# The skewed bias is loaded ahead of the queries, by every eighth partition; the layer norms' features move by 64 bytes, the first 128 in a tile of their own

## The chip, the cores and the metric

The kernel runs on one core of a Trainium2 chip. The metric is the device time of one execution in microseconds (us), the median of three runs. The profile comes from one more execution that the hardware profiler recorded. Its engines are PE (TensorE, matmuls; PEld is its weight loading), DVE (VectorE), ACT (ScalarE), POOL (GpSimd) and SP (SyncE, here only an issuer of DMAs).

## What is computed

One layer of a decoder trunk over 256 tokens of width 2048, in float32. Three steps, each followed by a layer norm of the scaled input plus the step's result:

```python
h = x
mix = hybrid_mixer(h, w_in, w_out, ...)            # S5 | stick-breaking | NSA heads, then w_out
h = layer_norm(ALPHA * h + mix, ln_g[0], ln_b[0])
xa = memory_cross_attention(h, mem, wq, wkv, wo)
h = layer_norm(ALPHA * h + xa, ln_g[1], ln_b[1])
ff = conv_ffn(h, ffn_w_up, conv_w, conv_b, ffn_w_down)   # 2048 -> 2 x 5632 -> 2048
h = layer_norm(ALPHA * h + ff, ln_g[2], ln_b[2])
```

Two places of it matter here. The 16 NSA heads add a relative-position bias to their scores before the softmax. It depends on query minus key and on the head alone:

```python
def head_bias(dist):
    return tab[t5_bucket(dist)].reshape(*dist.shape, n_g, n_r).transpose(2, 3, 0, 1)
s_w = einsum('bqgrd,bkgd->bgrqk', qb, kwb) * scale + head_bias(dist_w)
```

And the output of the first two layer norms is the input of the next projections: of `wq` (2048 to 512) and of `w_up` (2048 to 11264).

## The kernel before

**Products.** Every large product is taken in three matmuls of a rounded float32: a number is split into `hi` (rounded) and `lo` (the rest), and hi·hi, hi·lo and lo·hi are added up in PSUM. Weights come in chunks of 128 x 1024 (512 KB). SyncE loads each into `raw` (four buffers). ScalarE casts it to `hi` (L285), VectorE subtracts for `lo` (L286), with three buffers each. TensorE reads them in `mm3` (L300 to L302: hi with the high features, hi with the low ones, lo with the high ones), where the weights are the 128 x 128 stationary operand and 256 tokens of features the moving one. `mm3x` (L308 to L310) has the roles the other way round, features stationary and up to 512 weight columns moving. `to_rows` makes one tile of 128 outputs from two chunks: 16 blocks k of 128 features, 48 matmuls in a row. The up-projection is 88 such tiles, the query projection 4.

**Features.** In the mixer the features are the split input `A`. From the first layer norm on they are the four tiles mix0 to mix3, of four blocks each, high and low (`features`); block k is in tile k // 4. The names in rows leave the number out: all four read `mix`. The layer norms write them by `split_on_pe`: TensorE transposes 128 columns of the normalised rows into PSUM, ScalarE casts them (high), TensorE subtracts that in PSUM, ScalarE casts again (low). The same memory holds mixer outputs before, and kept weight chunks in the down-projection. Where a tile begins within a partition follows from the sizes of the pools in front of it. `gap` allocates a few bytes that nothing reads, to shift what comes after. hi and lo begin 32 bytes past a multiple of 128, mix0 and mix1 too, A, mix2 and mix3 96 past one.

**The skewed bias.** `g_dr` in DRAM holds for each head its bias as a row of 384 numbers over the distance. The slab is that bias for 128 queries at once, partition p shifted by p: 128 partitions x 16 heads x 256 numbers, 2 MB. Eight DMAs on ScalarE's queue (L962), each for 16 neighbouring partitions, load it at the start of `nsa`. There it gets memory of its own in a pool that opens after the S5 part is over. `nsa` goes over four quads of heads and two branches. For each head it multiplies queries `nq` with keys `kh`, `kl` (L995, L996), VectorE adds the slab in a reduction that gives the minimum too (L999, L1001, with `mn`), adds the bias of the compressed keys (`tcs`, L1007), and ScalarE takes the exponential (`pe`, L1011). Scores lie in `mx`, two PSUM buffers.

**Order.** A scheduler sets the order of instructions on each engine ahead of time. The program gives it lanes of priority (`lane`: "first", "split", "mixer", "proj", "late"), and `after` forces single pairs. So work of several phases is mixed: around 215 us the last S5 output matmuls (`pa` from `Es`, `Ec`), key projections (`kh`, L926) and, after them, the S5 gelu on `s5u` (L753), its split `s5zs` (L293), the gate product with `w_glu` (16 blocks of 3 matmuls on `s5zs`), then query projections (`nq`, L947). Each engine works its list strictly in order, and a DMA that waits on ScalarE's queue holds what stands behind it. DMAs of both queues take turns at eight completion semaphores, so that an issue also waits for the landing of the transfer that used its semaphore before.

## Time and profile before

| | us |
|---|---|
| median of three runs | 1310.14 (1310.13 to 1311.78) |
| the profiled execution | 1312.0 |
| its span in the trace | 1310.2 |
| PE busy | 1266.3 |
| DVE busy | 882.8 |
| ACT busy | 659.6 |
| DMA, mean over the span | 181 GB/s |

The span is the time from the first to the last instruction in the trace. Busy times of different engines overlap. A matmul's record runs from its start to its modelled end, longer than the distance to the next one; so a pace is read as the distance of starts. A row's last part, in brackets or behind the bar, is the time that the engine idled before it and what ended that. PEclk is the granted clock of TensorE as a share of full speed.

### The profile page before, as it was taken

How to read it: one execution, taken by the hardware profiler on the slowest of the kernel's cores; microseconds unless marked ns; L12 is line 12 of the kernel's file. 1: busy time of each engine (PE TensorE's matmuls, PEld its weight loads, DVE VectorE, ACT ScalarE, POOL GpSimd, SP SyncE). 2: the span in 40 equal slices, each digit the busy share in tenths (PEclk: the TensorE clock that was granted, in tenths of full speed). 3: DMA queues.
4: the chain of work that ended last, by engine and by line, in shares of the span. 5: the costliest groups of instructions: out<-in, count | busy, mean ns of one | idle time of the engine just before them, and what ended most of it. 6: DMA issues, size and time to landing. Idle time of an engine off the chain costs nothing.

```text
span 1310.2 us, 23007 instructions
## 1 busy us (share of the span) xinstructions
PE 1266.3 (97%) x9221; PEld 1172.5 (89%) x9221; DVE 882.8 (67%) x1510; ACT 659.6 (50%) x1030; POOL 13.3 (1%) x23
## 2 busy tenths in 40 slices
PE   7999999969999999899999999999999999999996
PEld 7788899958789899699999999999999988888896
DVE  7799998857774675866666666666666654554557
ACT  6884446446563355455554555554455443333342
POOL 0200000000000000000000000000000000000000
PEclk9999999979999999999999999999999999999998
DMA  8653346763456564445555555555555665556573
GB/s 299 192 168 122 99 144 211 166 154 130 129 178 221 181 214 140 135 147 191 192 183 190 193 184 187 192 186 186 191 190 185 238 208 193 193 193 192 183 238 129
DMA packets 68886, 237.37 MB, mean 181 GB/s; under 512 B 7787, under 2 KB 10652, under 8 KB 68012
## 3 DMA queue, kind: packets, MB, share of 16 engines
q1 hardware_dynamic: 64720, 230.21, 53.5%
q10 hardware_dynamic: 3276, 3.47, 1.8%
q0 software_dynamic: 784, 2.23, 0.9%
q8 instruction: 72, 1.18, 0.4%
q14 instruction: 34, 0.28, 0.1%
HBM read 231.82 MB, written 2.49 MB: 179 GB/s over the span
## 4 chain that ended last, share of the span: by engine, by line
PE 90%; DMA 3%; DVE 3%; ACT 2%; issue 1%; SPq 0%; ACTq 0%; DVEq 0%
PE pj L302 17%; PE pj L300 17%; PE pj L301 17%; PE pj L309 10%; PE pj L308 10%; PE pj L310 10%; PE pa L1032 2%; DMA raw<-in_win_u 2%; DMA slab<-g_dr 1%; PE pa L183 1%; PE mx L995 1%; DVE lo L286 1%; PE mx L996 1%; PE mx L865 1%; ACT hi L285 1%
## 5 line engine op out<-in xcount | busy, mean ns | idle before, releaser
L286 DVE TENSOR_TENSOR lo<-raw,hi 128x1024 fp32r<-128x1024 f32 (+2 forms) x403 | 488.4, 1212 | 350.3 <-ACT hi L285 349.1
L285 ACT CAST hi<-raw 128x1024 fp32r<-128x1024 f32 (+2 forms) x403 | 419.5, 1041 | 517.4 <-PE pj L301 291.2
L300 PE MATMUL pj<-mix,hi 128*128 128x256 f32 x1472 | 412.4, 281 | 0.8 <-ACT hi L285 0.8
L301 PE MATMUL pj<-mix,hi 128*128 128x256 f32 x1472 | 412.1, 280 | 0.0
L302 PE MATMUL pj<-mix,lo 128*128 128x256 f32 x1472 | 411.7, 280 | 0.0
L300 PEld LDWEIGHTS pj<-mix,hi 128*128 128x128 f32 x1472 | 279.4, 190 | 1.6 <-ACT hi L285 1.3
L301 PEld LDWEIGHTS pj<-mix,hi 128*128 128x128 f32 x1472 | 279.4, 190 | 0.2
L302 PEld LDWEIGHTS pj<-mix,lo 128*128 128x128 f32 x1472 | 279.2, 190 | 0.1
L300 PE MATMUL pj<-A,hi 128*128 128x256 f32 x496 | 140.0, 285 | 8.2 <-ACT hi L285 7.2
L302 PE MATMUL pj<-A,lo 128*128 128x256 f32 x496 | 139.1, 287 | 4.7 <-DVE lo L286 4.6
L301 PE MATMUL pj<-A,hi 128*128 128x256 f32 x496 | 138.8, 283 | 0.0
L300 PEld LDWEIGHTS pj<-A,hi 128*128 128x128 f32 x496 | 94.3, 191 | 10.6 <-ACT hi L285 8.1
L302 PEld LDWEIGHTS pj<-A,lo 128*128 128x128 f32 x496 | 93.1, 191 | 9.9 <-DVE lo L286 5.9
L309 PE MATMUL pj<-lo,act 128*128 128x512 f32 (+1 forms) x280 | 96.8, 347 | 0.0
L310 PE MATMUL pj<-hi,act 128*128 128x512 f32 (+1 forms) x280 | 96.8, 347 | 0.0
L309 PE MATMUL pj<-lo,A 128*128 128x512 f32 (+2 forms) x288 | 96.2, 335 | 0.0
L310 PE MATMUL pj<-hi,A 128*128 128x512 f32 (+2 forms) x288 | 95.6, 333 | 0.0
L301 PEld LDWEIGHTS pj<-A,hi 128*128 128x128 f32 x496 | 94.2, 191 | 0.8 <-issue 0.8
L308 PE MATMUL pj<-hi,A 128*128 128x512 f32 (+2 forms) x288 | 91.0, 334 | 0.0
L308 PE MATMUL pj<-hi,act 128*128 128x512 f32 (+1 forms) x280 | 89.7, 347 | 0.0
L309 PEld LDWEIGHTS pj<-lo,A 128*128 128x128 f32 x288 | 54.1, 188 | 6.5 <-issue 1.5
L309 PEld LDWEIGHTS pj<-lo,act 128*128 128x128 f32 x280 | 52.9, 189 | 6.6
(314 smaller groups left out, 1680.2 us busy)
## 6 DMA issues: line engine op xcount, KB each, us to landing
raw<-in_w_up SPq DMA_DIRECT2D x176, 512.0 KB, 4.2
raw<-in_w_down SPq DMA_DIRECT2D x92, 512.0 KB, 4.3
raw<-in_win_c SPq DMA_DIRECT2D x48, 512.0 KB, 4.0
raw<-in_w_out SPq DMA_DIRECT2D x32, 512.0 KB, 3.4
raw<-in_win_sv SPq DMA_DIRECT2D x8, 512.0 KB, 4.9
raw<-in_wk_m SPq DMA_DIRECT2D x8, 512.0 KB, 4.3
raw<-in_wv_m SPq DMA_DIRECT2D x8, 512.0 KB, 4.1
raw<-in_wq SPq DMA_DIRECT2D x8, 512.0 KB, 4.3
```

Source lines behind the costliest of these rows:

```text
L183: ins = getattr(self.engine, name)(*args, **kw)
L285: self.last_hi = nc.scalar.copy(hi[:, :n], raw[:, :n])
L286: self.last_lo = nc.vector.tensor_sub(lo[:, :n], raw[:, :n], hi[:, :n].bitcast(F32))
L300: mm(ps, hi, ah, start=start, stop=False)
L301: mm(ps, hi, al, start=False, stop=False)
L302: self.last_mm = mm(ps, lo, ah, start=False, stop=stop)
L308: mm(ps, ah, hi, start=start, stop=False)
L309: mm(ps, ah, lo, start=False, stop=False)
L310: self.last_mm = mm(ps, al, hi, start=False, stop=stop)
L865: mm(h_ps[:, 0:75].rearrange("p (g n) -> p g n", g=5), w1[:, i * 128:i * 128 + 128], kv[:, :, 2 * l:2 * l + 16 * NC_ - 15:16], start=l == ...
L995: mm(zs, q[:, t, gl, qs], kh[:, 0:m], start=True, stop=False)
L1032: ins = mm(o[64 * r:64 * r + 64, gl, 128 * c:256], vv[:, c, v, :], pt[:, k0:k1], start=start[r] is None, stop=False, skip_group_check=True)
```

## The change

The slab's load becomes a function of its own, `nsa_slab`, called ahead of `nsa_queries` with the first lane's priority. Its tile shares one buffer with `xraw` and `Es` (tag "Es", new pool `slabp`), so it can be written once the S5 output matmuls have read `Es`. DMA c fills partitions c, c + 8, c + 16 and so on; a source step is 376 numbers in place of 383. The 64-byte gap "m" is dropped, which moves all that is allocated behind it by 64 bytes: mix0 and mix1 (to 96 past a multiple of 128), `kh`, `kl`, `vv`; mix2 and mix3 stay at 96, and `nq`, A, hi and lo where they were. Feature block 0 gets a tile of its own, mixk, behind a new gap "k": it stands at 32. `split_features` writes block 0 apart where it comes in one group with others.

```diff
-    def __init__(self, *tiles):
-        self.tiles, self.n = tiles, tiles[0].shape[1]
+    def __init__(self, *tiles, first=None):
+        self.tiles, self.n, self.first = tiles, tiles[0].shape[1], first
 
     def __call__(self, k, i, q=slice(0, 256)):
-        return self.tiles[k // self.n][:, k % self.n, i, q]
+        return self.range(k, 1)[:, 0, i, q]
+
+    def range(self, k, n):
+        if k == 0 and self.first is not None:
+            assert n == 1
+            return self.first
+        return self.tiles[k // self.n][:, k % self.n:k % self.n + n]
...
         self.acts = pool("acts", 1)
-        self.gap("m", 64)
         self.stat = pool("stat", 2)
...
-        return [pool.tile([128, 4, 2, 256], F32R, name=f"mix{2 * i + j}")
-                for i, pool in enumerate((self.mixp, self.mixq)) for j in range(2)]
+        return Parts(*[pool.tile([128, 4, 2, 256], F32R, name=f"mix{2 * i + j}")
+                       for i, pool in enumerate((self.mixp, self.mixq)) for j in range(2)],
+                     first=self.hkp.tile([128, 1, 2, 256], F32R, name="mixk"))
...
-        raw = self.s5p.tile([128, KD, 256], F32, name="xraw", tag="Es")
+        raw = self.slabp.tile([128, KD, 256], F32, name="xraw", tag="Es")
...
             self.nsq = pool(nsa, "nsq", 1)
+            self.slabp = pool(nsa, "slabp", 1)
             with ExitStack() as s5:
...
+                self.nsa_slab()
                 self.nsa_queries()
                 self.nsa()
         self.mix_out(0)
         self.xkv = pool(self.xstack, "xkv", 1, "right")
+        self.gap("k", 64)
+        self.hkp = pool(self.ctx, "hkp", 1)
         self.gbp = pool(self.ctx, "gbp", 1)
...
-        Es = p.tile([128, 16, 256], F32, name="Es", tag="Es")
+        Es = self.slabp.tile([128, 16, 256], F32, name="Es", tag="Es")
...
+    def nsa_slab(self):
+        g_dr, n = self.g_dr, 128 // SKEW
+        self.nq = self.nsp.tile([128, 8, 2, 256], F32R, name="nq")
+        self.slab = self.slabp.tile([128, NH, 256], F32, name="slab", tag="Es")
+        with self.lane("first"):
+            for c in range(n):
+                src = bass.AP(g_dr.tensor, g_dr.offset + 127 - c,
+                              [[384 - n, SKEW], [SKEW * 384, NH], [1, 256]])
+                self.nc.scalar.dma_start(self.slab[c:128:n], src)
...
-        slab = p.tile([128, NH, 256], F32, name="slab")
-        for c in range(128 // SKEW):
-            src = bass.AP(g_dr.tensor, g_dr.offset + 127 - c * SKEW,
-                          [[383, SKEW], [SKEW * 384, NH], [1, 256]])
-            nc.scalar.dma_start(slab[c * SKEW:c * SKEW + SKEW], src)
+        slab = self.slab
...
+    def split_features(self, ps, H, k, n, q=slice(0, 256)):
+        if k == 0 and n > 1:
+            self.split_on_pe(ps[:, 0:1], H.range(0, 1)[..., q])
+            ps, k, n = ps[:, 1:], 1, n - 1
+        self.split_on_pe(ps, H.range(k, n)[..., q])
...
-                self.split_on_pe(ps.rearrange("p k t c -> p k (t c)"),
-                                 H[k // 4][:, k % 4:k % 4 + kk])
+                self.split_features(ps.rearrange("p k t c -> p k (t c)"), H, k, kk)
...
-                self.split_on_pe(ps, H[k // 4][:, k % 4:k % 4 + kk, :,
-                                               tok * 128:tok * 128 + 128])
+                self.split_features(ps, H, k, kk, slice(tok * 128, tok * 128 + 128))
...
-        keep = [t.rearrange("p k i t -> p (k i t)") for t in self.features()]
+        keep = [t.rearrange("p k i t -> p (k i t)") for t in self.features().tiles]
```

On ScalarE, at the S5 output and at the queries, the list of before is this (`slab<-g_dr` is a load of 16 partitions, `nq` the queries, `hi` a weight chunk; the brackets name semaphores waited for):

```order
L947 ACTIVATE nq<-pj 64x256 [waits Activation_49]
L947 ACTIVATE nq<-pj 64x256 [waits PE_49]
L962 DMA slab<-g_dr 16x16x256
L285 CAST hi<-raw 128x1024 [waits DMAHW1_49,PE_49]
L962 DMA slab<-g_dr 16x16x256 x4
L947 ACTIVATE nq<-pj 64x256 [waits DVE_49]
L962 DMA slab<-g_dr 16x16x256 [waits DMAHW2_49]
L285 CAST hi<-raw 128x1024 [waits PE_49,Activation_49]
```

The last two loads follow behind two more query casts. The list of after is this, some forty instructions earlier (L938 is the line of `kh`, L765 the gelu on `s5u`, L979 the gate):

```order
L938 CAST kh_2091<-pj 64x2x128 [waits DVE_49]
L938 CAST kh_2091<-pj 64x2x128
L962 DMA slab<-g_dr 16x16x256 [waits PE_49]
L962 DMA slab<-g_dr 16x16x256 x3
L962 DMA slab<-g_dr 16x16x256 [waits DMAHW6_49]
L962 DMA slab<-g_dr 16x16x256 [waits DMAHW7_49]
L962 DMA slab<-g_dr 16x16x256 [waits DMAHW0_49]
L962 DMA slab<-g_dr 16x16x256 [waits DMAHW1_49]
L291 CAST hi<-raw 128x1024 [waits PE_49,Activation_49] x2
L938 CAST kh_2091<-pj 64x2x128 x2
L765 ACTIVATE s5u<-s5u 128x1024 [waits DVE_49]
L253 ACT_TABLE_LOAD
```

The eight loads have moved from between the query casts to behind the key casts, ahead of the gelu. The first waits for TensorE, the last four each for a DMA's completion.

On VectorE, where the first scores meet the slab, the list of before is this (`lo` is a weight chunk's low part, `tt` the scores with the bias):

```order
L948 SCALAR_TENSOR_TENSOR nq<-pj,nq 64x256 [waits Activation_49] x2
L286 TENSOR_TENSOR lo<-raw,hi 128x1024 [waits DMAHW1_49,PE_49,Activation_49]
L948 SCALAR_TENSOR_TENSOR nq<-pj,nq 64x256 [waits Activation_49]
L286 TENSOR_TENSOR lo<-raw,hi 128x1024 [waits DMAHW2_49,PE_49,Activation_49]
L948 SCALAR_TENSOR_TENSOR nq<-pj,nq 64x256 [waits Activation_49] x3
L286 TENSOR_TENSOR lo<-raw,hi 128x1024 [waits DVE_49,DMAHW3_49,PE_49,Activation_49]
L999 ISA tt,mn<-mx,slab 128x128 [waits DMAHW3_49,DMAHW4_49,DMAHW2_49,DMAHW5_49,DMAHW1_49,DMAHW7_49,DMAHW0_49,DVE_49]
L999 ISA mn 128x1
L1001 ISA tt,mn<-mx,slab 128x256
```

and of after (L1015 is the line of the first bias addition):

```order
L300 TENSOR_TENSOR mix_2535<-s5z,mix_2535 128x256 [waits Activation_49]
L971 SCALAR_TENSOR_TENSOR nq<-pj,nq 64x256 [waits Activation_49] x2
L292 TENSOR_TENSOR lo<-raw,hi 128x1024 [waits DMAHW1_49,PE_49,Activation_49]
L1015 ISA tt,mn<-mx,slab 128x128 [waits DVE_49,PE_49]
L1015 ISA mn 128x1
L1017 ISA tt,mn<-mx,slab 128x256
L1017 ISA mn 128x1
L1023 TENSOR_TENSOR tcs_3328<-mx,slab 128x7
```

The first `tt` has lost its seven waits for DMAs and stands ahead of two more chunks' `lo` and four queries' steps instead of behind them.

On TensorE, from the last block of one tile of the up-projection to the first of the next, before (the numbers are those of buffers):

```order
L300 MATMUL pj_7796<-mix3_5932,hi_7829 128x256
L301 MATMUL pj_7796<-mix3_5932,hi_7829 128x256
L302 MATMUL pj_7796<-mix3_5932,lo_7830 128x256
L300 MATMUL pj_7865<-mix0_5929,hi_7868 128x256
L301 MATMUL pj_7865<-mix0_5929,hi_7868 128x256
L302 MATMUL pj_7865<-mix0_5929,lo_7869 128x256
```

and after, from the last block of one tile to the second of the next:

```order
L306 MATMUL pj_7272<-mix3_5940,hi_7305 128x256
L307 MATMUL pj_7272<-mix3_5940,hi_7305 128x256
L308 MATMUL pj_7272<-mix3_5940,lo_7306 128x256
L306 MATMUL pj_7341<-mixk_5941,hi_7344 128x256
L307 MATMUL pj_7341<-mixk_5941,hi_7344 128x256
L308 MATMUL pj_7341<-mixk_5941,lo_7345 128x256
L306 MATMUL pj_7341<-mix0_5937,hi_7344 128x256
L307 MATMUL pj_7341<-mix0_5937,hi_7344 128x256
L308 MATMUL pj_7341<-mix0_5937,lo_7345 128x256
```

Block 0 comes from mixk now, and mix0 gives blocks 1 to 3; the order of matmuls is as it was.

## Rows read from the trace of the kernel before

**Rows 1.** The page's busy times of the engines

```profile
PE 1266.3 (97%) x9221; PEld 1172.5 (89%) x9221; DVE 882.8 (67%) x1510; ACT 659.6 (50%) x1030; POOL 13.3 (1%) x23
```

**Rows 2.** The page's costliest groups: line, engine, operation, count, busy us, mean ns, idle before, releaser

```profile
L286 DVE TENSOR_TENSOR lo<-raw,hi 128x1024 fp32r<-128x1024 f32 (+2 forms) x403 | 488.4, 1212 | 350.3 <-ACT hi L285 349.1
L285 ACT CAST hi<-raw 128x1024 fp32r<-128x1024 f32 (+2 forms) x403 | 419.5, 1041 | 517.4 <-PE pj L301 291.2
L300 PE MATMUL pj<-mix,hi 128*128 128x256 f32 x1472 | 412.4, 281 | 0.8 <-ACT hi L285 0.8
```

**Rows 3.** Waits from 240 to 280 us: who waits, for what; us, times, longest us

```profile
ACT pe L1011 <- DVE mn L999: 16.2, 1, 16.2
DVE tt L999 <- DMA slab<-g_dr: 14.5, 1, 14.5
...
PE mx L995 <- DVE tcs L1007: 12.5, 1, 12.5
...
DVE lo L286 <- ACT hi L285: 2.2, 4, 0.9
```

**Rows 4.** The chain of waits, 240 to 285 us: start us, us, what

```profile
254.01 19.50 DMA slab<-g_dr
```

**Rows 5.** Two stretches: us, busy us of each engine, PEclk, DMA share, GB/s

```profile
262.00:274.80 12.80, 0.32 (x3) 0.12 (x2) 0.93 (x9) 0.53 (x3) 0.00 (x0) 0.63 1.01 187
274.80:279.00 4.20, 4.18 (x19) 4.20 (x20) 3.73 (x21) 4.13 (x11) 0.00 (x0) 0.50 0.20 41
```

**Rows 6.** Timeline of TensorE behind the idle stretch: start us, us, engine, instruction

```profile
276.05 0.41 PE L300 MATMUL pj<-A,hi 128*128 128x256 f32 x1
276.27 0.41 PE L301 MATMUL pj<-A,hi 128*128 128x256 f32 x1
```

**Rows 7.** The slab's tile: its DMA issues, duration ns min/median/max, and their landings

```profile
L962 ACTq DMA_DIRECT2D slab<-g_dr x8: 328/490/1851, 247.8 to 254.0; - x8
...
DMA to landing us min/median/max: 6.0/13.3/19.5
```

**Rows 8.** Timeline of TensorE: the last readers of `Es`

```profile
214.03 0.80 PE L183 MATMUL pa<-Es,s5c 128*32 128x256 f32 x5
```

**Rows 9.** Timeline of ScalarE, 212 to 232 us

```profile
214.28 0.75 ACT L926 CAST kh<-pj 64x256 fp32r<-64x256 f32 x2
215.94 1.06 ACT L753 ACTIVATE s5u<-s5u 128x1024 f32<-128x1024 f32 x1 [0.91 <-DVE s5u L183]
...
218.50 1.04 ACT L285 CAST hi<-raw 128x1024 fp32r<-128x1024 f32 x1
...
220.33 1.05 ACT L293 CAST s5zs<-s5u 128x1024 fp32r<-128x1024 f32 x1
```

**Rows 10.** Timeline of TensorE in one tile of the up-projection

```profile
705.50 0.28 PE L300 MATMUL pj<-mix,hi 128*128 128x256 f32 x1
...
706.22 0.29 PE L300 MATMUL pj<-mix,hi 128*128 128x256 f32 x1
...
706.57 0.28 PE L300 MATMUL pj<-mix,hi 128*128 128x256 f32 x1
...
706.91 0.28 PE L300 MATMUL pj<-mix,hi 128*128 128x256 f32 x1
...
707.59 0.28 PE L300 MATMUL pj<-mix,hi 128*128 128x256 f32 x1
```

**Rows 11.** Timeline of TensorE with the activations A as moving operand

```profile
212.11 0.28 PE L300 MATMUL pj<-A,hi 128*128 128x256 f32 x1
...
213.13 0.28 PE L300 MATMUL pj<-A,hi 128*128 128x256 f32 x1
...
216.05 0.28 PE L300 MATMUL pj<-A,hi 128*128 128x256 f32 x1
...
217.11 0.28 PE L300 MATMUL pj<-A,hi 128*128 128x256 f32 x1
```

**Rows 12.** Timeline of TensorE: the first gate matmul

```profile
228.42 0.28 PE L300 MATMUL pj<-s5zs,hi 128*128 128x256 f32 x1
```

More of the change, by code (lines that the diff above doesn't have):

```diff
@@ L433, in run @@
         self.layer_norm(H)
-        self.cross_attention(Parts(*H))
-        self.ffn(Parts(*self.H))
+        self.cross_attention(H)
+        self.ffn(self.H)
     def features(self):
-        return [pool.tile([128, 4, 2, 256], F32R, name=f"mix{2 * i + j}")
-                for i, pool in enumerate((self.mixp, self.mixq)) for j in range(2)]
+        return Parts(*[pool.tile([128, 4, 2, 256], F32R, name=f"mix{2 * i + j}")
+                       for i, pool in enumerate((self.mixp, self.mixq)) for j in range(2)],
+                     first=self.hkp.tile([128, 1, 2, 256], F32R, name="mixk"))
     def load_x(self):
         nc, a, S = self.nc, self.a, self.nc.scalar
-        raw = self.s5p.tile([128, KD, 256], F32, name="xraw", tag="Es")
+        raw = self.slabp.tile([128, KD, 256], F32, name="xraw", tag="Es")
         self.s5u = u = self.s5p.tile([128, 4, 256], F32, name="s5u")
@@ L937, in nsa_keys @@
                                 ps[64 * gl:64 * gl + 64].rearrange("p (g c k) -> p g c k", g=1, c=2))
+    def nsa_slab(self):
[7 more added lines that the diff above has]
+                self.nc.scalar.dma_start(self.slab[c:128:n], src)
     def nsa_queries(self):
-        a, V, S, p = self.a, self.nc.vector, self.nc.scalar, self.nsp
-        q = p.tile([128, 8, 2, 256], F32R, name="nq")
+        a, V, S, q = self.a, self.nc.vector, self.nc.scalar, self.nq
         for t in range(8):
@@ L949, in nsa_queries @@
                                        q[own, t, gl, :].bitcast(F32), ALU.mult, ALU.subtract)
-        self.nq = q
     def nsa(self):
@@ L956, in nsa @@
         vcb, vv, gate, ks, q = self.vcb, self.vv, self.gate, self.ks, self.nq
-        g_dr = self.g_dr
-        slab = p.tile([128, NH, 256], F32, name="slab")
-        for c in range(128 // SKEW):
-            src = bass.AP(g_dr.tensor, g_dr.offset + 127 - c * SKEW,
-                          [[383, SKEW], [SKEW * 384, NH], [1, 256]])
-            nc.scalar.dma_start(slab[c * SKEW:c * SKEW + SKEW], src)
+        slab = self.slab
         self.after(S.activation(gate, gate, ACTF.Exp, scale=-1.0), self.table)
```

## The prediction, made before the changed kernel ran

> **What bounds the kernel now.** I read the page's busy times first: TensorE works for 97% of the span, so a change counts only where it removes an idle stretch of TensorE or makes its matmuls follow each other faster [rows 1]. The costliest groups then say who feeds whom: ScalarE's casts (`hi`) mostly wait for TensorE to let go of a buffer, VectorE's `lo` waits for `hi`, and the matmuls of the feature tiles hardly wait (0.8 us over 1472) [rows 2]. Both feeders have slack on average, so idle stretches had to be looked for one by one.
>
> The waits of 240 to 280 us show the one large stretch: VectorE's first bias addition waits 14.5 us for the slab, the exponential on ScalarE behind it 16.2 us, and TensorE idles 12.5 us, because its next scores need a PSUM buffer that VectorE hasn't read [rows 3]. The chain of waits agrees: the step that ended last there is the slab's last transfer, issued at 254.01 and 19.50 us long [rows 4]. [...]
>
> For the second half of the change I read starts of successive matmuls instead of their durations (0.28 us each, overlapping). In a tile of the up-projection, 16 feature blocks times 3 matmuls, the first eight blocks come from mix0 and mix1, the last eight from mix2 and mix3. From 705.50 to 706.22, in mix1, six matmuls take 0.72 us, 120 ns each. From 706.91 to 707.59, in mix2, six take 0.68 us, 113.3 ns each [rows 10]. Same engine, same clock, same shapes, no wait: what differs is the address. mix0 and mix1 stand 32 bytes past a multiple of 128 in a partition, mix2 and mix3 stand 96 past one, and hi and lo stand at 32. Of two operands with the same 64-byte phase the pace is 120 ns, of two with different phase 113.3 ns.
>
> **The change part by part.** *The slab's wait.* Issued behind the last S5 output matmuls, which end about 215 [rows 8], the eight transfers have some 40 us: VectorE's wait of before began 14.5 us ahead of 254.01 + 19.50, at 259, and it now asks a few us sooner. Even the 19.50 us of the slowest would be done by 235 [rows 3, 4]. So the idle 12.5 us go. The clock's loss goes with them: 4.2 us in which each matmul takes 0.22 us instead of 0.118 [rows 5, 6, 11], so 4.2 x 0.46 = 1.9 us. Together 14.4 us. What is late next there is the ordinary pace of matmuls: VectorE now does the first scores ahead of two `lo` steps instead of behind them, in the pattern that the rest of the attention already has; I put 0 to 1 us on that, within the last term below.
>
> *What the earlier issue costs.* It puts eight DMA issues on ScalarE's queue ahead of two casts, the S5 gelu, its table load, the gate and the cast of `s5zs`. An issue alone is 0.33 us [rows 7], but the fifth to eighth wait for landings: three for weight loads already under way, the eighth for the slab's own first piece. Every cast behind it waits too. Call L the time from the first issue to that landing. ScalarE is free for the first issue at 214.28 + 0.75 = 215.03 and is released at 215.03 + L + 0.33 = 215.36 + L. Then follow two `hi` (2.1 us), `kh` (0.75), gelu to gate (218.50 - 215.94 = 2.56), `hi` (1.05), `kh` (0.75), `s5zs` (1.05) and VectorE's low part (1.2): 9.46 us in all [rows 2, 9]. TensorE wants that low part in its second gate matmul, at 228.42 + 0.12 = 228.54 [rows 12]. So it stalls for 215.36 + L + 9.46 - 228.54 = L - 3.7 us. Before, the landing took 6.0 us at least and 19.5 at most [rows 7]. I take 6.0, since that first piece also went out with none of the others ahead of it: a stall of 2.3 us. Bounds: none (L up to 3.7) and 9.6 (L at the median 13.3). The first chunk behind the issues is less tight: 2.4 us after release, wanted 5.6 us before 228.5, which asks L above 5.2.
>
> The weight loads are moved past the slab too: three later loads on SyncE wait for the second to fourth piece to land. Their chunks are wanted after the four gate tiles, 48 matmuls or 5.6 us behind 228.42 [rows 12], at 234, and a landing at 222 leaves 12 us for a load and its split; I cost it at nothing, and with L over 10 it would add to the stall. GpSimd's queue doesn't change. Two norm-parameter loads move by one weight load: nothing.
>
> The source step of the new pattern also spreads each piece over every eighth partition. [...]
>
> *The features' move.* After it mix0 to mix3 all stand at 96, against hi and lo at 32, and only block 0, in its own tile, stands at 32. The 1472 matmuls of each kind are 92 tiles of 16 blocks [rows 2]: 88 of the up-projection and 4 of the query projection. Before, a tile is 24 x 120 + 24 x 113.3 = 5600 ns. After, if the pace after block 0 returns to 113.3, it is 3 x 120 + 45 x 113.3 = 5460 ns: 140 ns less, 12.9 us over 92 tiles. The matmuls next to a change of phase aren't yet at the steady pace: the three from 706.22 take 0.35 us, not 0.34 [rows 10]. I take off 0.7 us for such edges: 12.2 us.
>
> That "if" is the weak step. Different phases alone don't settle the pace. The activations A stand at 96 too, against hi at 32, and run at 113.3 ns in one stretch (nine matmuls from 212.11 to 213.13, 1.02 us) and at 117.8 ns in another (216.05 to 217.11, 1.06 us), with the S5 matmuls between them [rows 11]. So there are two steady paces, and how the run is entered chooses. For the fast one: each change from mix1 to mix2 in this trace goes to it, 92 tiles alike. Against: there 24 matmuls at the slow pace come first, and after the change just three.
>
> *The rest.* Other operands change phase as well: the mixer output's blocks, the kept chunks of the down-projection, the key tiles. Some 200 matmuls get or lose up to 6.7 ns each [rows 10], so -1.3 to +1.3 us; I take 0. Two more casts and one more matmul in the layer norms, from block 0's own tile, lie beside the residual matmuls; the first tile after the norm needs block 0 first, and it is cast first.
>
> **The sum.** The profiled span is 1310.2 us, its own time 1312.0; the median of three runs is 1310.14, and I take the differences off the median: 1310.1 - 14.4 + 2.3 - 12.2 = **1285.8 us**. Its own range: 1281 (no stall, 12.9 for the features, -1.3 for the rest) to 1290 (a stall of 5).
>
> **The rivals.** *The pace of 117.8 ns holds after block 0.* Then a tile takes 3 x 120 + 45 x 117.8 = 5661 ns, 61 more than before, +5.6 us over 92: 1310.1 - 14.4 + 2.3 + 5.6 = **1303.6 us**. For it: the A stretch at 117.8 [rows 11]. Against it: the entries from mix1.
>
> *The move does nothing, or half.* The rows show the same two paces in each tile, and these go with the address [rows 10]; but an effect of the tile itself, its place in the buffer or its position in the accumulation, would look the same, and the move wouldn't reach that. Time: 1310.1 - 14.4 + 2.3 = **1298.0 us**; with some tiles at each pace, (-12.2 + 5.6) / 2, **1294.8**. [...]
>
> *Slower than before: ScalarE is held by the landing.* The mechanism is the stall above, with L as its price, and 1.9 us of half clock as after the idle stretch of before. It undoes the slab's 14.4 from L - 3.7 + 1.9 = 14.4, L = 16.2 us, where the features give nothing, and from 28.4 where they give 12.2. At before's largest landing, 19.5 [rows 7], it is 1310.1 - 14.4 + 17.7 = **1313.4 us** without the features' gain. Against it: that landing was the last of a queue of eight; the one waited for is the first.
>
> *The slab isn't what is waited for last.* If TensorE idled at the first scores for another reason, the gain would shrink; but the 14.5 us end with the transfer, and VectorE's next largest sum of waits there is 2.2 us in four pieces [rows 3].
>
> **How the numbers follow.** Forecast 0.55; the pace of 117.8 ns 0.22; nothing or half 0.16; held past the gain 0.04; other, near no change 0.03. A measurement of this kernel can tell about 0.2%, 2.6 us. The range takes the forecast's own low end, 1281, and the pace of 117.8 ns with a little to spare, 1304; outside lie a larger stall on top of that pace, and the slower case. Faster 0.92, same 0.03, slower 0.05.
>
> **What would show it.** Slab: VectorE's row of the wait for the slab is gone, TensorE's largest idle stretch between 240 and 280 is under 1 us, and no clock of 0.50 stands there. Stall: around 228 TensorE waits about 2 us for VectorE's `s5zs`, and ScalarE shows an idle stretch from 215 to 221. Features: the starts in a tile go 120 for three matmuls, then 113.3; a steady 117.8 is the first rival, an unchanged half and half the second. The prediction is wrong if the time is over 1290, and then the starts in a tile say whether it is the features, and the idle stretch near 228 whether it is the stall.

## The result

The changed kernel takes 1294.34 us (median; 1293.75 to 1295.49) against 1310.14 (1308.28 to 1311.78): a ratio of 0.9877, 95% interval 0.9865 to 0.9888, 15.8 us less. That is inside the range (1281 to 1304) and 8.5 us above the forecast of 1285.8, but over the 1290 at which the forecast's own range ends. It is also 0.5 us from the time that the prediction gave to a rival in which the features' move does half. The trace shows that this rival is not what happened.

The busy times of after, from the page, answer to [rows 1]; TensorE has lost 11.7 us of busy time.

```profile
span 1292.0 us, 23010 instructions
...
PE 1254.6 (97%) x9222; PEld 1160.8 (90%) x9222; DVE 883.8 (68%) x1510; ACT 659.9 (51%) x1032; POOL 13.3 (1%) x23
```

**Where the time went, by stage.** The starts of the same TensorE instructions in both timelines:

| event on TensorE | before, us | after, us | difference |
|---|---|---|---|
| last S5 output matmul | 214.5 | 214.0 | -0.5 |
| first gate matmul (s5zs) | 228.4 | 233.6 | +5.1 |
| last gate matmul | 234.3 | 241.9 | +7.6 |
| first matmul on the features (query projection) | 474.9 | 468.9 | -6.1 |
| last matmul of the up-projection | 1056.0 | 1037.5 | -18.5 |
| last matmul of all | 1299.0 | 1280.8 | -18.2 |

The features' part, from the query projection on, gave 12.4 us; the prediction had 12.2. The slab's part gave 5.6 us (from -0.5 to -6.1); the prediction had 14.4 - 2.3 = 12.1. So the whole miss lies between 214 and 469 us. (The spans differ by 18.2 and the medians by 15.8, since the profiled execution of before was a long one: 1312.0.)

**The features.** The timeline of TensorE in one tile of after, beside [rows 10]: block 0 (`mixk`) at 704.60 and again at 710.06, and six matmuls in the middle.

```profile
704.60 0.28 PE L306 MATMUL pj<-mixk,hi 128*128 128x256 f32 x1
...
706.66 0.28 PE L306 MATMUL pj<-mix,hi 128*128 128x256 f32 x1
...
707.34 0.28 PE L306 MATMUL pj<-mix,hi 128*128 128x256 f32 x1
...
710.06 0.28 PE L306 MATMUL pj<-mixk,hi 128*128 128x256 f32 x1
```

A tile takes 5.46 us instead of 5.60, and six matmuls take 0.68 us, 113.3 ns each. At 706.66 the tile is still in mix1, which ran at 120 ns before.

**The slab.** Its wait on VectorE is gone. In its place the waits of after from 205 to 260 us, beside [rows 3], show ScalarE held for 9.0 us, and TensorE waiting for what stands behind that on ScalarE and VectorE. The waits of 2.2 and 0.8 us are for the first weight chunk behind the issues; the 2.0 us are for a gate tile's result, which ScalarE reads out of PSUM late (`s5z`). For `s5zs` TensorE doesn't wait:

```profile
ACT hi L291 <- DMA slab<-g_dr: 9.0, 1, 9.0
...
PE pj L306 <- ACT hi L291: 2.2, 1, 2.2
...
PE pj L306 <- ACT s5z L782: 2.0, 1, 2.0
...
PE pj L308 <- DVE lo L292: 0.8, 1, 0.8
```

The timeline of ScalarE, beside [rows 9], shows the hold itself: the eight issues take from 214.40 to 223.50, and the cast that stood at 218.50 starts at 223.59. The rows on the slab's tile give the landings, beside [rows 7]: 8.5 us at least, where the prediction had 6.0.

```profile
214.40 9.10 ACTq L962 DMA_DIRECT2D slab<-g_dr  x8
223.59 1.99 ACT L291 CAST hi<-raw 128x1024 fp32r<-128x1024 f32 x2 [9.04 <-DMA slab<-g_dr]
```

```profile
L962 ACTq DMA_DIRECT2D slab<-g_dr x8: 540/630/1221, 214.4 to 223.0; - x8
...
DMA to landing us min/median/max: 8.5/10.3/12.2
```

Four stretches of after (length, busy times of PE, PEld, DVE, ACT and POOL, granted clock, DMA share, GB/s) show what followed. TensorE did 1.0 us of work from 222 to 226 and then for most of the next 4 us its matmuls followed each other by 0.214 us instead of 0.118 (granted clock 0.57 in the mean). A second loss came at the first scores: TensorE waited 3.0 us for VectorE's query step, the row behind them says, and the granted clock fell again, to 0.51.

```profile
222.00:226.00 4.00, 1.00 (x7) 0.59 (x6) 1.33 (x2) 2.37 (x4) 0.00 (x0) 1.00 1.12 199
226.00:230.00 4.00, 4.00 (x21) 4.00 (x22) 2.35 (x5) 3.95 (x6) 0.00 (x0) 0.57 1.11 205
259.00:263.60 4.60, 1.62 (x14) 1.43 (x13) 4.44 (x18) 3.92 (x13) 0.00 (x0) 1.00 0.61 192
263.60:267.10 3.50, 3.50 (x19) 3.50 (x18) 2.37 (x13) 0.99 (x4) 0.00 (x0) 0.51 0.16 67
```

```profile
PE mx L1011 <- DVE nq L971: 3.0, 1, 3.0
```

### The profile page after: what moved, and what is told of

Read it like the earlier page. It is cut to its first block, busy times and chain, and to the rows that moved or that the text cites. A ratio compares the mean times of both kernels' runs of the same rounds, so it can differ in the third digit from the quotient of the medians.

```text
span 1292.0 us, 23010 instructions
## 1 busy us (share of the span) xinstructions
PE 1254.6 (97%) x9222; PEld 1160.8 (90%) x9222; DVE 883.8 (68%) x1510; ACT 659.9 (51%) x1032; POOL 13.3 (1%) x23
## 4 chain that ended last, share of the span: by engine, by line
PE 76%; DVE 3%; ACT 1%; issue 1%; DMA 0%; DVEq 0%; ACTq 0%
PE pj L306 14%; PE pj L307 14%; PE pj L308 14%; PE pj L314 9%; PE pj L316 9%; PE pj L315 9%; PE pa L1048 2%; DVE lo L292 1%; PE mx L1011 1%; PE mx L1012 1%; DVE R L1144 1%; DVE R L1149 1%; PE op L1041 0%; PE pb L1041 0%; ACT hi L291 0%
## 5 line engine op out<-in xcount | busy, mean ns | idle before, releaser
L307 PE MATMUL pj<-mix,hi 128*128 128x256 f32 x1380 | 381.9, 277 | 0.0
L306 PE MATMUL pj<-mix,hi 128*128 128x256 f32 x1380 | 381.1, 277 | 0.0
L308 PE MATMUL pj<-mix,lo 128*128 128x256 f32 x1380 | 381.0, 276 | 0.0
L307 PEld LDWEIGHTS pj<-mix,hi 128*128 128x128 f32 x1380 | 259.2, 188 | 0.1
L308 PEld LDWEIGHTS pj<-mix,lo 128*128 128x128 f32 x1380 | 259.2, 188 | 0.1
L306 PEld LDWEIGHTS pj<-mix,hi 128*128 128x128 f32 x1380 | 259.1, 188 | 0.2
L306 PEld LDWEIGHTS pj<-A,hi 128*128 128x128 f32 x496 | 95.9, 194 | 11.2 <-ACT hi L291 9.3
L307 PEld LDWEIGHTS pj<-A,hi 128*128 128x128 f32 x496 | 96.1, 194 | 1.9 <-issue 1.9
```

The costliest lines, as they stand in the source:

```text
L306: mm(ps, hi, ah, start=start, stop=False)
L307: mm(ps, hi, al, start=False, stop=False)
L308: self.last_mm = mm(ps, lo, ah, start=False, stop=stop)
```

## The experiments

Every kernel was run beside the kernel before on its own chip, so ratios to before are compared; "us" is the ratio times 1310.14.

| run | edit | median, us | ratio to before, interval | "us" |
|---|---|---|---|---|
| changed kernel | | 1294.34 | 0.9877 (0.9865 to 0.9888) | 1294.0 |
| e1_slab_only | slab part alone | 1306.88 | 0.9961 (0.9946 to 0.9976) | 1305.0 |
| e2_features_only | features' part alone | 1299.51 | 0.9906 (0.9891 to 0.9922) | 1297.8 |
| e3_no_own_tile | block 0 back in mix0 | 1309.80 | 0.9987 (0.9975 to 0.9999) | 1308.4 |
| e4_own_tile_at_96 | block 0's own tile at 96 | 1310.50 | 0.9989 (0.9978 to 0.9999) | 1308.7 |
| e5_four_loads | four loads of 32 partitions | 1285.22 | 0.9800 (0.9785 to 0.9814) | 1283.9 |
| e6_neighbours | early, pattern of before | 1298.11 | 0.9903 (0.9883 to 0.9923) | 1297.4 |
| e7_gpsimd_eight | eight loads, GpSimd's queue | 1289.36 | 0.9829 (0.9814 to 0.9845) | 1287.7 |
| e8_gpsimd_four | four loads, GpSimd's queue | 1284.49 | 0.9793 (0.9779 to 0.9808) | 1283.0 |
| e9_A_own | e8, block 0 of A apart too | 1306.95 | 0.9968 (0.9955 to 0.9981) | 1305.9 |
| e10_pattern_only | before, new pattern alone | 1305.53 | 0.9958 (0.9944 to 0.9972) | 1304.6 |
| e11_k_128_further | e8, block 0 128 bytes on | 1287.56 | 0.9808 (0.9792 to 0.9825) | 1285.0 |
| e12_mix_128_further | e8, mix0, mix1 128 bytes on | 1301.82 | 0.9926 (0.9909 to 0.9942) | 1300.4 |

My theory after the comparison was that the features' step had been right and the hold of ScalarE had been sized too small. The rival was the even split that the total suggests: the features gave half, and the slab all of its gain.

### The two parts apart

The slab part alone (from the changed kernel):

```diff
         self.acts = pool("acts", 1)
+        self.gap("m", 64)
...
-                       for i, pool in enumerate((self.mixp, self.mixq)) for j in range(2)],
-                     first=self.hkp.tile([128, 1, 2, 256], F32R, name="mixk"))
+                       for i, pool in enumerate((self.mixp, self.mixq)) for j in range(2)])
...
-        self.gap("k", 64)
-        self.hkp = pool(self.ctx, "hkp", 1)
```

> Slab part alone: early load and every eighth partition, features at the addresses of before. In the changed kernel's trace the up-projection became 11.7 us shorter (TensorE's first to last matmul on the features minus what was gained before it) and the rest of the gain, some 6 us, lies before the first layer norm. If the two parts simply add: 1294.3 + 12 = 1306 us, that is 4 us faster than before, with ScalarE held some 9 us behind the slab's first piece, and a tile of the up-projection at 5.60 us. Rival: the 64 bytes also speed up the attention (key tiles, mixer output), then the slab alone is worth less: 1308 to 1310.

The features' part alone (not shown: the pool `slabp` goes too, and `nq` is allocated where it was before):

```diff
-                self.nsa_slab()
                 self.nsa_queries()
...
-        slab = self.slab
+        g_dr = self.g_dr
+        slab = p.tile([128, NH, 256], F32, name="slab")
+        for c in range(128 // SKEW):
+            src = bass.AP(g_dr.tensor, g_dr.offset + 127 - c * SKEW,
+                          [[383, SKEW], [SKEW * 384, NH], [1, 256]])
+            nc.scalar.dma_start(slab[c * SKEW:c * SKEW + SKEW], src)
```

> Features' move alone, with block 0 in its own tile; the slab is loaded as before, late and by 16 neighbours. If the parts add: 1310.1 - 12 = 1298 us, VectorE still waits some 14.5 us for the slab, a tile of the up-projection takes 5.46 us. If the move also helps the attention: 1294 to 1297.

The slab alone is worth 5.1 us, the features alone 12.3; together 17.4 against 16.1 of both at once. The intervals reach 1.5 us to each side or more, so the parts add. In the first, ScalarE is held as in the changed kernel and TensorE waits behind it; in the second VectorE and TensorE wait at least as long as before (the waits put it down to `raw`, one of several DMAs waited for together). Waits of the first from 205 to 260 us, and of the second from 240 to 280:

```profile
ACT hi L292 <- DMA slab<-g_dr: 9.9, 1, 9.9
...
PE pj L307 <- ACT hi L292: 3.2, 1, 3.2
```

```profile
DVE tt L1019 <- DMA raw<-in_win_c: 15.7, 1, 15.7
...
PE mx L1015 <- DVE tcs L1027: 14.0, 1, 14.0
```

So the split of the miss is settled: the rival, an even split, is out.

### What chooses the pace of the features

Block 0 back in mix0, its tile allocated but unused:

```diff
+        self.hkp.tile([128, 1, 2, 256], F32R, name="mixk")
         return Parts(*[pool.tile([128, 4, 2, 256], F32R, name=f"mix{2 * i + j}")
-                       for i, pool in enumerate((self.mixp, self.mixq)) for j in range(2)],
-                     first=self.hkp.tile([128, 1, 2, 256], F32R, name="mixk"))
+                       for i, pool in enumerate((self.mixp, self.mixq)) for j in range(2)])
```

> The changed kernel, with block 0 in mix0 as before (its own tile is allocated but unused, so that nothing else moves): all 16 blocks stand at 96, hi and lo at 32. Theory, two steady paces and the entry chooses: without the three matmuls at the other phase nothing sets the pace anew, and a tile runs at 117.8 ns throughout, 48 x 117.8 = 5654 ns against 5457, so 1294.3 + 88 x 0.197 = 1312 us. Rival, different phase alone gives the fast pace: 48 x 113.3 = 5438 ns, 1294.3 - 88 x 0.019 = 1292.6 us.

Block 0 in its own tile, but at 96:

```diff
-        self.gap("k", 64)
         self.hkp = pool(self.ctx, "hkp", 1)
+        self.gap("k", 64)
```

> The changed kernel with the 64-byte gap behind block 0's tile instead of ahead of it: block 0 keeps a tile of its own, but at 96 like the other 15, nothing else moves. Theory, the phase of block 0 sets the pace of the whole tile: all 48 matmuls at 117.7 ns as in the run without the tile, up-projection 17 us longer than in the changed kernel, total 1308 to 1311 us. Rival, a tile of its own is what does it (another place in memory, whatever its phase): 113.3 ns and 1294 us.

The groups of TensorE from 600 to 1000 us, one row of each kernel: the changed one, e3, e4. Count over blocks is the number of tiles in 400 us.

```profile
L306 PE MATMUL pj<-mix,hi 128*128 128x256 f32 x1099 | 303.8, 276 | 0.0
```

```profile
L306 PE MATMUL pj<-mix,hi 128*128 128x256 f32 x1133 | 318.4, 281 | 0.0
```

```profile
L306 PE MATMUL pj<-mix,hi 128*128 128x256 f32 x1062 | 298.4, 281 | 0.0
```

The changed kernel has 15 such blocks a tile (block 0 reads `mixk`): 400 / (1099 / 15) = 5.46 us. Without the tile there are 16: 400 / (1133 / 16) = 5.65 us, 117.7 ns a matmul. With the tile at 96, 15 again: 400 / (1062 / 15) = 5.65 us. Both runs lose 14.4 us or more against the changed kernel and end within 0.3% of before. So it isn't the 64-byte move that gains: with all 16 blocks at 96 the whole tile runs at the pace that I had as the first rival. Three matmuls of block 0 at the weights' phase bring the other 45 to 113.3. And it is block 0's phase that does it, not a tile of its own.

### What the early slab costs

Four loads of 32 partitions, every fourth, so that no issue waits for another landing:

```diff
-SKEW = 16
+SKEW = 32
```

> The changed kernel with four slab loads of 32 partitions (every fourth) in place of eight of 16: none of the four issues has to wait for the landing of a transfer before it on the same completion semaphore, so ScalarE isn't held. Theory, the hold is what was mis-sized: TensorE's waits of 2.4, 0.9, 0.7 and 2.2 us from 222 to 237 go, and 1.5 us of half clock with them: 1294.3 - 7 = 1287 us. If VectorE's backlog before the first scores (TensorE's 3.2 us at 259 and its half clock) comes from the hold as well: 1282 to 1284. Rival, TensorE waits there for weight loads that share the DMA queues with the slab: the waits stay, with a DMA as their end, and the time is within 2 us of 1294.

Eight early loads with the pattern of before:

```diff
-                src = bass.AP(g_dr.tensor, g_dr.offset + 127 - c,
-                              [[384 - n, SKEW], [SKEW * 384, NH], [1, 256]])
-                self.nc.scalar.dma_start(self.slab[c:128:n], src)
+                src = bass.AP(g_dr.tensor, g_dr.offset + 127 - c * SKEW,
+                              [[383, SKEW], [SKEW * 384, NH], [1, 256]])
+                self.nc.scalar.dma_start(self.slab[c * SKEW:c * SKEW + SKEW], src)
```

> The changed kernel with the pattern of before: eight early loads on ScalarE, each of 16 neighbouring partitions. Theory, the spread over partitions makes the packets quick (mean of one 1 KB packet: 145 ns before, 90 in the changed kernel, 52 with every fourth partition), and the hold is the landing of the first piece: packets near 145 ns, the hold of 9.0 us grows by some 4 to 6, and TensorE's stall with it: 1298 to 1302 us. Rival, the hold is set by the number of loads under way, not by their spread: within 1.5 us of 1294.

The same eight, or the four, from GpSimd's queue:

```diff
-                self.nc.scalar.dma_start(self.slab[c:128:n], src)
+                self.nc.gpsimd.dma_start(self.slab[c:128:n], src)
```

> The changed kernel with the same eight loads issued from GpSimd's queue, which has nothing else to do there. Theory, ScalarE held is the whole of the stall: TensorE's waits of 6.2 us between 222 and 237, the 3.2 us at 259 and two stretches of half clock (1.5 us each) all go: 1294.3 - 12 = 1282 us. Rival, the weight loads are slowed by the slab's traffic as well, and TensorE waits for these: 1287 to 1292 us, with a DMA of raw as the end of a wait.

> Both at once: four loads of every fourth partition from GpSimd's queue. Theory, neither ScalarE is held nor do packets take long: 1281 to 1283 us, and not more than 1 us from the eight loads on the same queue, since nobody waits for the slab by then. Rival, traffic of the slab delays the weight loads: the quicker packets make it 2 to 4 us faster than the eight loads.

With four loads on ScalarE 10 us come back. The timeline of ScalarE shows a shorter hold, 214.22 to 219.84, where I had expected none: no issue waits for a landing, but the last one itself took 3.56 us, for a reason that the trace doesn't show. The waits of TensorE from 214 to 300 us are 2.5 us in all:

```profile
214.22 5.62 ACTq L962 DMA_DIRECT2D slab<-g_dr  x4
219.96 1.05 ACT L291 CAST hi<-raw 128x1024 fp32r<-128x1024 f32 x1 [5.58 <-PE pj L308]
```

```profile
PE pj L306 <- DVE kl L939: 1.4, 2, 0.8
PE pj L308 <- DVE lo L292: 0.8, 1, 0.8
PE pj L306 <- ACT hi L291: 0.3, 1, 0.3
```

The wait of 3.0 us at the first scores is gone too, and neither stretch of half clock stands there. It is gone in the runs from GpSimd's queue as well. But the lists, not the hold, account for it. In the changed kernel TensorE goes from the first eight score matmuls straight to the next four, and the query step (`nq`) that these need stands on VectorE behind the bias additions of the first eight and a chunk's `lo`. In the runs without the wait (e5, e7, e8) that step stands ahead of the first bias addition, and TensorE has 24 matmuls of a query projection between the scores. VectorE's timeline in the changed kernel, then in e5:

```profile
259.31 0.29 DVE L1015 CUSTOM_DVE_ANT_0 tt<-mx,slab 128x128 f32<-128x128 f32 x1
...
261.90 0.43 DVE L971 SCALAR_TENSOR_TENSOR nq<-pj,nq 64x256 fp32r<-64x256 f32 x1
```

```profile
254.60 0.43 DVE L971 SCALAR_TENSOR_TENSOR nq<-pj,nq 64x256 fp32r<-64x256 f32 x1
255.05 0.29 DVE L1015 CUSTOM_DVE_ANT_0 tt<-mx,slab 128x128 f32<-128x128 f32 x1
```

Four kernels have the changed kernel's order there: ScalarE stood 8.0, 9.0, 9.3 and 9.9 us at the slab (e3, the changed kernel, e4, e1), and TensorE's wait at the first scores is 2.95 to 2.98 us in all four. So this second loss goes with the order of the lists, and in e5, e7 and e8 the scheduler made another one. Why it did, and what the order is worth alone, no run shows. Nor does the wait settle whether the half clock follows: it did in the changed kernel and in e1, and did not in e3 and e4 (the stretch behind the wait in e3, granted clock 1.00):

```profile
262.30:266.50 4.20, 4.20 (x38) 4.20 (x37) 4.00 (x21) 2.14 (x6) 0.00 (x0) 1.00 0.27 94
```

Eight loads from GpSimd's queue free ScalarE of the hold, and yet cost 4.7 us more than four (0.9829 against 0.9793; the intervals, 0.9814 to 0.9845 and 0.9779 to 0.9808, lie apart). Their waits from 210 to 265 us show the rival of that run: ScalarE waits for weights, TensorE behind it. With four loads TensorE's only wait from 214 to 300 us is 0.6 us.

```profile
ACT hi L291 <- DMA raw<-in_win_c: 5.8, 2, 4.5
...
PE pj L306 <- ACT s5z L782: 3.0, 1, 3.0
```

```profile
PE pj L306 <- DVE kl L939: 0.6, 1, 0.6
```

Two rows of the same stretch, eight loads and then four, show why (the last number is GB/s): at the same full share of the DMA engines the four move more.

```profile
218.00:222.00 4.00, 4.00 (x37) 4.00 (x36) 3.32 (x5) 3.93 (x7) 1.43 (x3) 1.00 1.03 237
```

```profile
218.00:222.00 4.00, 4.00 (x37) 4.00 (x36) 3.80 (x5) 3.90 (x8) 0.00 (x0) 1.00 1.03 369
```

The run with neighbours early, e6, is a half miss. It lost some 3 us against the changed kernel (the intervals just overlap), the low end of what was forecast, but not by a longer hold: ScalarE is held 7.5 us instead of 9.0. TensorE's long wait is again behind weights that came late. Waits from 210 to 265 us:

```profile
ACT hi L291 <- DMA slab<-g_dr: 7.5, 1, 7.5
...
PE pj L306 <- ACT s5z L782: 5.4, 1, 5.4
ACT hi L291 <- issue: 5.2, 3, 2.1
ACT hi L291 <- DMA raw<-in_win_c: 3.5, 1, 3.5
```

What the spread does is seen in the slab's queue alone. Rows of the DMA queues (packets, MB, share of 16 engines): before and e10 (below: every eighth, issued as late as before) from 240 to 280 us; then from 205 to 240 us e6 (neighbours), the changed kernel (every eighth), e5 (every fourth).

```profile
q10 hardware_dynamic: 2176, 2.10, 47.1%
```

```profile
q10 hardware_dynamic: 2176, 2.10, 26.8%
```

```profile
q10 hardware_dynamic: 2176, 2.10, 41.1%
```

```profile
q10 hardware_dynamic: 2176, 2.10, 33.4%
```

```profile
q10 hardware_dynamic: 2112, 2.10, 19.0%
```

Share times 16 engines times the window over packets, a few short ones counted in: 139 ns a packet before (0.471 x 16 x 40 us / 2176) and 79 with the pattern alone changed; 106 for neighbours early, 86 for every eighth, 50 for every fourth. So at either place of the issue a packet took less by every eighth partition than by neighbours, and in the four loads by every fourth less again; what makes it so, no run shows. The shortest landing did not get shorter with it: 8.5 us by every eighth partition, 7.2 by neighbours (e6). In both, several pieces were under way together; no run sends one alone.

The pattern alone, at the late place of before:

```diff
-            src = bass.AP(g_dr.tensor, g_dr.offset + 127 - c * SKEW,
-                          [[383, SKEW], [SKEW * 384, NH], [1, 256]])
-            nc.scalar.dma_start(slab[c * SKEW:c * SKEW + SKEW], src)
+            src = bass.AP(g_dr.tensor, g_dr.offset + 127 - c,
+                          [[376, SKEW], [SKEW * 384, NH], [1, 256]])
+            nc.scalar.dma_start(slab[c:128:8], src)
```

> The kernel before with the pattern alone: the slab is issued as late as before, but by every eighth partition. Theory, the spread makes a packet take some 90 ns instead of 145, so the eight transfers, which take the DMA queues some 23 us from first packet to last, end some 4 to 7 us sooner and VectorE's 14.5 us shrink by as much: 1304 to 1307 us. Rival, the transfers are limited by the rate at which ScalarE issues them (the last at 254) and by the weight loads beside them: within 2 us of before.

As its theory said, 5.5 us, from the waits of 240 to 280 us: 7.4 us on VectorE and 4.1 on TensorE, where before had 14.5 and 12.5.

```profile
DVE tt L999 <- DMA raw<-in_win_c: 7.4, 1, 7.4
...
PE mx L995 <- DVE tcs L1007: 4.1, 1, 4.1
```

So the pattern alone is worth as much as the whole slab part of the change, 5.5 and 5.1 us. Early, without a hold and in the order of e8 the slab is worth e8 less e2, (0.9906 - 0.9793) x 1310.14 = 14.8 us.

### How far the rule of the pace reaches

The e8 run with block 0 of the activations A in its own tile too. For its 2 KB, 128 bytes of the gap ahead of A were given up.

```diff
-        self.gap("a", 192)
+        self.gap("a", 64)
...
-        self.X = Parts(self.Xt)
+        self.X = Parts(self.Xt, first=self.consts.tile([128, 1, 2, 256], F32R, name="Ak"))
...
```

> The four loads from GpSimd, and now the rule of the features is put on the activations A as well: their block 0 gets a tile of its own at 32, the other 15 stay at 96. In the run with the four loads from GpSimd, 451 of some 1234 steady steps between matmuls with A as moving operand are at 117 to 119 ns, 783 at 113. Theory, the first block's phase sets the pace: nearly all go to 113, 451 x 4.4 ns = 2 us off 1284.5: 1282.5 us. Rival, it works only where a tile's 48 matmuls run without others between them: the shares stay near where they are, and the time within 1 us.

It lost 23 us against e8, neither theory. All features ran at the slow pace: 400 / (1061 / 15) = 5.65 us a tile, from 600 to 1000 us. So did nearly all of A: of some 1320 steady steps between its matmuls 1180 are at 116 to 119 ns, against 472 in e8.

```profile
L306 PE MATMUL pj<-mix,hi 128*128 128x256 f32 x1061 | 297.0, 280 | 0.0
```

The places modulo 128 were those of the changed kernel. Modulo 256 they weren't: hi and lo begin at 32 in both, but A, mix0 and mix1 had gone from 224 to 96, and block 0's tile from 32 to 160; mix2 and mix3 stayed at 224. Two runs took these apart. Block 0's tile alone, 128 bytes on:

```diff
-        self.gap("k", 64)
+        self.gap("k", 192)
         self.hkp = pool(self.ctx, "hkp", 1)
+        self.gap("l", 128)
```

> The run with four loads from GpSimd, with block 0's tile 128 bytes further on (at 160 past a multiple of 256 in place of 32) and 128 bytes of gap behind it, so that all else keeps its place modulo 256. hi and lo begin at 32 past a multiple of 256, blocks 1 to 15 at 224. Seen so far: with A's own block the whole program had moved by 2048 or by 1920 bytes, block 0's tile stood at 160, and all tiles ran at 117.8 ns although the 64-byte phases were those of the changed kernel. Theory, the place of block 0 counts modulo 256: all 48 matmuls at 117.7 ns, 1284.5 + 17 = 1301.5 us. Rival, modulo 128 is enough and something else in that run (mix0 and mix1 at 96 past a multiple of 256) held the pace: 113.3 ns and 1284.5 us.

mix0 and mix1, 128 bytes on, block 0 at 32:

```diff
         self.acts = pool("acts", 1)
+        self.gap("m", 128)
...
-        self.gap("k", 64)
+        self.gap("k", 192)
```

> The run with four loads from GpSimd, with mix0, mix1 and what lies behind them 128 bytes further on, and 128 more in the gap ahead of block 0's tile: mix0 and mix1 stand at 96 past a multiple of 256 in place of 224, block 0 again at 32, mix2 and mix3 at 224, hi and lo at 32. Block 0 at 160 alone left the fast pace nearly as it was (5.50 us a tile), so in the run with A's own block something else kept all tiles at 117.8 ns. Theory, it is mix0's and mix1's place modulo 256, 64 bytes past hi's instead of 64 ahead of it: 117.8 ns again, 1284.5 + 17 = 1301 us. Rival, it was both together, or the whole program's move by 2048 bytes: 113.3 ns and 1284 to 1287 us.

The groups from 600 to 1000 us, block 0's tile moved, then mix0 and mix1 moved:

```profile
L306 PE MATMUL pj<-mix,hi 128*128 128x256 f32 x1094 | 303.1, 277 | 0.0
```

```profile
L307 PE MATMUL pj<-mix,hi 128*128 128x256 f32 x1063 | 298.1, 280 | 0.0
```

The first gives 5.48 us a tile, near the fast pace, and 1285.0 us; my theory for it fell. The second gives 5.64 us and 1300.4 us, as its theory said. So of the places tried, mix0 and mix1 must stand at 224 past a multiple of 256, that is 64 bytes short of the weights' place; with these two 64 bytes past it, the whole tile keeps 117.7 ns, mix2 and mix3 at 224 too, even with block 0 at the weights' phase. That A ran slowly in e9 for the same reason fits, but wasn't tried by itself.

## Why the prediction was right in its range and off in its middle

**The wait for the slab: right.** 14.4 us were forecast for taking it away; e8 against e2 measures 14.8 where nothing is held. VectorE's wait for the slab and the half clock behind it are gone in the trace. The prediction's sign also asked for no idle stretch of TensorE over 1 us and no clock of 0.50 between 240 and 280 us; 3.0 us and 0.51 stand there, from the order of the lists.

**The features: right, term and condition.** 12.2 us forecast, 12.4 in the trace and 12.3 by e2. The weak step, "if the pace after block 0 returns to 113.3", held. The first rival's pace is real: e3 and e4 show it, when block 0 is not at the weights' phase.

**The cost of the earlier issue: right in kind, too small in its size.** This is the step that failed: the term L - 3.7, taken as 2.3 us, and the 0 to 1 us for the first scores. It had three faults.

- L itself. I took 6.0, the smallest landing of before, because that piece went out ahead of the others. In the changed kernel four pieces are issued back to back, and none landed in less than 8.5 us. By the formula that is 4.8 us of stall instead of 2.3. Nor did TensorE wait at `s5zs` "around 228", as the sign said: it stood between 222 and 226 at the first chunk behind the issues, which I had called less tight and put at L above 5.2. L - 5.2 is 3.3 us, and 2.2 + 0.8 were measured. The other kernels with this order agree: L is 7.5, 8.8 and 9.3 us in e3, e4 and e1, and these waits are 2.0, 3.0 and 3.7.
- What a stall brings with it. I put 1.9 us of half clock on the idle stretch of before and on the slower rival, but none on my own stall. Behind it 15 matmuls followed each other by 0.214 us instead of 0.118: an estimated 1.4 us. And 2.0 us more of waiting for ScalarE, whose list was still late, came at the gate.
- The new order at the first scores. I had 0 to 1 us there; it was a wait of 3.0 us, the same in four kernels with different holds, and an estimated 1.5 us of half clock behind it.

These come to 3.0 + 1.4 + 2.0 + 3.0 + 1.5 = 10.9 us, and the changed kernel less e8 is 11.0 by the ratios. That is close to the 2.3 us of the forecast and the 8.5 us by which it missed.

The slower rival named the right place, ScalarE held by the landing. Between the forecast and a loss of all the slab's gain no case had a price of its own: the bounds of the stall went to 9.6 us, but the forecast's range took one of 5.

**"I cost it at nothing", for the weight loads.** This cover is thinner than I had it. In e7, with no hold on ScalarE, weights were late and TensorE waited 3.0 us; four loads by every fourth partition take that away.

**The rival of half the gain** was close in time and wrong: e1 and e2, with one part each, tell it apart. (Its 1294.8 should read 1294.7: 1298.0 less 3.3.)

**The range held by luck.** Over 1290 us the prediction was to count as wrong, and the time is over it. The range went on to 1304 for the pace of 117.8 ns alone, and that didn't come; what came in its place was the larger stall and the order of the lists.

## What to carry to other kernels

A transfer moved off the critical path must also be moved off a queue on which others wait: an issue can be held by the landing of an earlier transfer on the same completion semaphore, and all that engine's work stands behind it (9.0 us of ScalarE here). Price such a stall with its consequences, the half clock behind it and the backlog on the engine: 2.3 us forecast were some 6.4 in the end. And read the new lists up to the next wait: those of after had the first bias additions ahead of four query steps before anything ran, and one of these steps is what TensorE waited for, some 4.5 us with its half clock. Four wider loads, from either queue, and the order that came with them took nearly all of it back (e8: 0.9793 of before). And when a total lands on a rival's number, look at the stage before believing it.

## What the hardware showed that I had not expected

- The pace of matmuls with 128 x 128 weights and 256 moving columns was 113.3, 117.7 or 120 ns here by where the two operands begin in a partition, and the first blocks of a tile can set it for the rest: block 0 at the weights' place, the others 64 bytes short of it modulo 256, gives 113.3; mix0 and mix1 64 bytes past it (e12), or block 0 with all the others (e3, e4), gives 117.7. That is up to 6% (120 against 113.3 ns) with the same shapes and no waits; what makes it was not found.
- A packet of the slab took 139, 106, 86, 79 or 50 ns in the mean by the place of its transfer in time and the partitions that it spreads over. Eight loads by every eighth partition also held back the weights' queue more than four by every fourth: 237 against 369 GB/s in all at the same share of the DMA engines (1.03), and ScalarE waited up to 4.5 us for weights (e7).
- The same wait of TensorE, 2.95 to 2.98 us in four kernels (in the changed one behind matmuls 0.12 us apart), was followed by a stretch at a granted clock of 0.51 and 0.50 in two kernels (the changed one, e1) and of 1.00 in two others (e3, e4).
- Spreading wide did not bring the first piece sooner: the shortest landing was 8.5 us by every eighth partition and 7.2 by neighbours, while the longest was 12.2 and 14.2.
